# Gate and up blocks of a SwiGLU layer by seven products that add up inside PSUM, the third product of each made during the next block

## The chip, the cores and the metric

The kernel runs on one core of one Trainium2 chip. The metric is device microseconds per execution, the median of three runs; lower is better. Matrix products run on TensorE (PE), elementwise work on VectorE (DVE) and ScalarE (ACT), a few small steps on GpSimd (POOL), and SyncE (SP) issues the loads. PE writes into PSUM, eight banks of 128 x 512 float32; DVE and ACT read them from there.

## The reference

One transformer layer on 512 rows of width 1024 in float32: a token mixer of two kinds of attention, a cross attention into 256 memory rows, and a SwiGLU feed-forward layer (FFN), each between two RMS norms and added to the residual. The change is in the FFN:

```python
D_FF = -(-8 * D_MODEL // 768) * 256          # 2816

def swiglu(h, w_gate_up, w_down):
    g, u = jnp.split(h @ w_gate_up, 2, axis=-1)
    return (jax.nn.silu(g) * u) @ w_down

        h = rms_norm(x, g_ffn_pre[l])
        x = x + rms_norm(swiglu(h, w_gate_up[l], w_down[l]), g_ffn_post[l])
```

## The kernel before

**Precision.** PE multiplies a rounded float32 format. Each operand is therefore split into a high part (a copy that rounds, on ACT) and a low part (the rest, a subtraction on DVE), and each product is three matmuls: high by high, high by low, low by high.

**Stages.** The FFN comes last, from about 425 us on. The normalised input stands transposed in `bt`, as blocks b11, b21, b12, b22 (two halves of the 1024 inner rows by two halves of the 512 rows of x), high and low. The 5632 columns of `w_gate_up` are done in 22 times two pieces of 128 columns each: block n is a gate block if n is even and an up block if odd, of 256 columns (two pieces m), and u = n // 2 counts pairs. Pair 0 comes from weights loaded earlier (`first_ffn`). Blocks 2 to 21 take their weights from a ring in SBUF. Then the down projection runs, first for the left 512 output columns, then for the right; five of its eleven items per half (`SEVEN`, items 4 to 8) are done by seven products too.

**One block.** A block is a 2 x 2 product: weights a11, a21, a12, a22 (two inner halves by two pieces of 128 columns) with b11 to b22. Directly that is eight products of 12 matmuls of 128 x 256 (`eight`). Strassen's scheme in Winograd's form does it with seven (`seven`), with sums of weights s1 to s4 (made on DVE for each block, L951 to L954) and sums of inputs t1 to t4 (made once, L1137 to L1144). Blocks 2, 3 and 11 are done by eight products, the other 17 by seven. In `seven` each of the seven products ends in PSUM by itself, in four banks, two halves each; ACT copies one of them to SBUF (`v`, L1155), and five additions on DVE (L1161, L1162, L1167, L1169, L1171) make the four outputs. Silu runs on ACT piece by piece for a gate block (L1176), and for an up block DVE multiplies with the gate (L1181, L1183). For u of 1, 2, 3 and 10 `keep` then splits the result (ACT L1062, DVE L1063); for the others the split is put off to the down projection (`late_seven`, L1217 to L1225).

**The ring.** `load_raw` brings a raw piece (512 KB, tile `fraw`, three buffers) by a DMA that SP issues when a buffer is free. `fill_from` writes the high part into `ring_hi` (ACT, L924) and the low part into `ring_lo` (DVE, L925). `take` fills ahead as far as the ring's slots allow, and so casts and splits of the next block stand between the sums of this one. Each engine runs its instructions in order.

**Order.** A scheduler gives each engine's instructions their order when the program is built. A split of the first product's matmuls into two halves of 128 columns (`IN_STEP`) is made at u of 1, 2, 4, 6, 8 and 10.

## Time and profile before

| | |
|---|---|
| median of 3 runs | 774.65 us (774.26 to 774.91) |
| profiled execution, first to last instruction | 771.6 us, granted TensorE clock 0.998 |
| PE, DVE, ACT busy | 755.6, 600.3, 429.4 us |
| gate/up blocks from the ring | 455.18 to 648.94 us |
| down projection and the end | 648.94 to 771.60 us |

The profile is of one execution; its span is 3.05 us under the median of the runs, which also count what lies before its first and behind its last instruction. A row of a timeline gives start, duration, engine, line, operation, output and inputs with their shapes; in brackets stands the idle time of the engine just before and what ended it. A matmul's duration includes its way through the array, so the distance of starts, not the duration, says how fast matmuls follow each other. Durations on DVE and ACT overlap a little in the same way.

### The profile page before, as it was taken

To read this page: it belongs to the slowest core of one execution; us is meant where nothing else is said; L and a number is where in the kernel's file an instruction comes from. 1 tells how busy PE (TensorE), PEld (TensorE's weight loads), DVE (VectorE), ACT (ScalarE), POOL (GpSimd) and SP (SyncE) were. 2 spreads that over 40 slices of the span, in tenths; PEclk is the share of its full clock that TensorE was granted. 3 is DMA by queue.
4 is the path that set the end of the run, shared out by engine and by line. 5 is a ranking of instruction groups with operands and counts; after the bars stand their busy time and mean duration, and the time that the engine had idled before them with its cause. 6 is when DMAs were issued, how large, how long until landed. Compare 5 with 4: busy or idle time off the path is not lost.

```text
span 771.6 us, 12900 instructions
## 1 busy us (share of the span) xinstructions
PE 755.6 (98%) x5012; PEld 677.0 (88%) x5012; DVE 600.3 (78%) x1098; ACT 429.4 (56%) x784; POOL 62.5 (8%) x105
## 2 busy tenths in 40 slices
PE   9999999999999999999999999999999999999996
PEld 9977888887778988877778999999999999898985
DVE  8668889789886688545653779999899998987746
ACT  7558889567874457444553625554444446553421
POOL 1001132100321210000002100000000000000001
PEclk9999999999999999999999999999999999999999
DMA  7522023422313725311340202332433332233312
GB/s 273 139 70 68 28 56 97 123 82 82 109 56 112 267 98 197 120 54 56 131 143 27 83 28 83 110 110 82 138 110 110 110 110 90 102 112 108 106 59 109
DMA packets 60749, 80.05 MB, mean 104 GB/s; under 512 B 2705, under 2 KB 43665, under 8 KB 60689
## 3 DMA queue, kind: packets, MB, share of 16 engines
q1 hardware_dynamic: 59264, 74.49, 29.9%
q0 software_dynamic: 1280, 4.72, 1.7%
q8 instruction: 39, 0.64, 0.3%
q14 instruction: 22, 0.17, 0.1%
q10 hardware_dynamic: 144, 0.02, 0.0%
HBM read 77.13 MB, written 2.10 MB: 103 GB/s over the span
## 4 chain that ended last, share of the span: by engine, by line
PE 79%; DVE 9%; ACT 6%; issue 3%; DMA 2%; POOL 1%; DVEq 0%; POOLq 0%; ACTq 0%
PE ps_a L144 12%; PE ps_a L146 12%; PE ps_a L143 12%; PE ps_a L1094 3%; PE ps_a L1097 3%; PE ps_a L1095 3%; PE ps_s L1097 3%; PE ps_s L1094 3%; PE ps_s L1095 3%; PE ps_s L143 2%; PE ps_s L144 2%; PE ps_s L146 2%; PE ps_t L552 2%; PE ps_o L561 2%; PE ps_s L533 1%
## 5 line engine op out<-in xcount | busy, mean ns | idle before, releaser
L924 ACT CAST ring_hi<-fraw 128x1024 fp32r<-128x1024 f32 (+1 forms) x62 | 57.2, 932 | 61.0 <-DVE fraw L1003 17.0
L126 DVE TENSOR_TENSOR lo<-raw,hi 128x1024 fp32r<-128x1024 f32 x56 | 68.2, 1224 | 20.5 <-ACT hi L125 20.3
L925 DVE TENSOR_TENSOR ring_lo<-fraw,ring_hi 128x1024 fp32r<-128x1024 f32 (+1 forms) x62 | 66.5, 1075 | 17.4 <-ACT ring_hi L924 17.1
L146 PE MATMUL ps_a<-hTh,lo 128*128 128x512 f32 x192 | 76.6, 399 | 0.0
L144 PE MATMUL ps_a<-hTl,hi 128*128 128x512 f32 x192 | 75.9, 395 | 0.0
L143 PE MATMUL ps_a<-hTh,hi 128*128 128x512 f32 x192 | 75.8, 395 | 0.0
L125 ACT CAST hi<-raw 128x1024 fp32r<-128x1024 f32 x56 | 57.8, 1048 | 25.3 <-PE ps_a L144 21.2
L924 ACT CAST ring_hi<-sums 128x1024 fp32r<-128x1024 f32 x34 | 35.7, 1049 | 35.5 <-PE ps_t L1095 10.2
L925 DVE TENSOR_TENSOR ring_lo<-sums,ring_hi 128x1024 fp32r<-128x1024 f32 x34 | 41.4, 1219 | 2.1 <-ACT ring_hi L924 2.1
L144 PEld LDWEIGHTS ps_a<-hTl,hi 128*128 128x128 f32 x192 | 36.1, 188 | 6.4
L146 PEld LDWEIGHTS ps_a<-hTh,lo 128*128 128x128 f32 x192 | 36.1, 188 | 6.3
L143 PEld LDWEIGHTS ps_a<-hTh,hi 128*128 128x128 f32 x192 | 36.2, 188 | 5.7
L547 ACT ACTIVATE p<-p,nm 128x128 f32<-128x128 f32 (+1 forms) x64 | 36.1, 565 | 8.1 <-DVE nm L537 7.2
L1094 PE MATMUL ps_a<-b,ring_hi 128*128 128x256 f32 x140 | 39.1, 279 | 0.0
L1097 PE MATMUL ps_a<-b,ring_lo 128*128 128x256 f32 (+1 forms) x146 | 39.0, 274 | 0.0
L1095 PE MATMUL ps_a<-b,ring_hi 128*128 128x256 f32 x140 | 38.7, 276 | 0.0
L1097 PE MATMUL ps_s<-b,ring_lo 128*128 128x256 f32 x128 | 35.3, 276 | 0.0
L1095 PE MATMUL ps_s<-b,ring_hi 128*128 128x256 f32 x128 | 35.3, 276 | 0.0
L1094 PE MATMUL ps_s<-b,ring_hi 128*128 128x256 f32 x128 | 35.3, 276 | 0.0
L554 ACT CAST pth<-ps_t 128x128 fp32r<-128x128 f32 (+1 forms) x64 | 27.0, 424 | 14.5 <-PE ps_t L552 13.7
L555 DVE TENSOR_TENSOR ptl<-ps_t,pth 128x128 fp32r<-128x128 f32 (+1 forms) x64 | 30.7, 487 | 5.0 <-ACT pth L554 3.8
L552 PE MATMUL ps_t<-ident,p 128*128 128x128 f32 x160 | 28.1, 275 | 1.1 <-DVE p L549 0.8
(552 smaller groups left out, 2630.5 us busy)
## 6 DMA issues: line engine op xcount, KB each, us to landing
raw<-in_dram SPq DMA_DIRECT2D x64, 512.0 KB, 3.7
fraw<-in_dram SPq DMA_DIRECT2D x62, 512.0 KB, 3.5
cb<-in_dram SPq DMA_DIRECT2D x8, 256.0 KB, 2.5
xo<-in_dram POOLq DMA_DIRECT2D x4, 512.0 KB, 7.5
out_dram<-yd SPq DMA_DIRECT2D x8, 256.0 KB, 2.0
rawv<-in_dram SPq DMA_DIRECT2D x3, 520.0 KB, 6.5
xt<-in_dram SPq DMA_DIRECT2D x3, 512.0 KB, 6.6
gb<-in_dram POOLq DMA_DIRECT2D x3, 512.0 KB, 4.4
```

What stands on the lines that cost most here:

```text
L125: act.copy(hi[:, j : j + n, :], raw)
L126: dve.tensor_tensor(out=lo[:, j : j + n, :], in0=raw, in1=f32(hi[:, j : j + n, :]), op=ALU.subtract)
L143: pe.matmul(dst, sh, mh, start=first, stop=False)
L144: pe.matmul(dst, sh, ml, start=False, stop=False)
L146: pe.matmul(dst[:, to], sl, mh[:, to], start=False, stop=last)
L547: act.activation(p[:, :n], p[:, :n], AF.Exp, bias=nm, scale=-1.0, accum_out=sm)
L552: pe.transpose(tp[:, k * P : (k + 1) * P], p[:, k * P : (k + 1) * P], ident)
L924: act.copy(h2, v)
L925: dve.tensor_tensor(out=l2, in0=v, in1=f32(h2), op=ALU.subtract)
L1094: pe.matmul(dst, w[0][:, k, :], b[:, 0, k, :], start=first and k == 0, stop=False)
L1095: pe.matmul(dst, w[0][:, k, :], b[:, 1, k, :], start=False, stop=False)
L1097: pe.matmul(dst[:, to], w[1][:, k, :], b[:, 0, k, to], start=False, stop=last and k == 3)
```

## The change

Two more blocks (3 and 11) are done by seven products; only block 2 is still done by eight. That makes 19 of the blocks from the ring where there were 17.

In a block by seven products three of them are now added to each other inside PSUM. The bank x takes a11 b11; ACT copies it out (`early`, L1178); then s2 t2 is added in place; ACT copies the new value (L1184); then s3 t3 is added, and ACT copies that too (u3, L1191). Two products, with t4 and t1, share a bank p45 and b21's product has a bank p2. One addition on DVE (L1192) gives the two outputs of the right half. The seventh product (s4 by b22) is added to p45 one block later, in `finish_seven`, ahead of that block's last product; two additions on DVE (L1168, L1169) then give the two outputs of the left half. `done(0)` and `keep` of a block therefore also come during the next one. For the last block the finishing product stands in the down projection's first item, behind t = 1. The sums t1 to t4 are written in the program ahead of the first pair, no longer behind it. The early copies of a gate block go to a spare row tile (`rrow`), those of an up block to `U[:, :, 0]`, which the up block before it fills its results into for u of 1, 2, 3.

The order of the weights in the ring changes with it: a11, the raw upper half, s2 with s1, then s4 of the block before with s3.

```diff
         def seven_weights(n, c0):
             raw, total = {}, sums[:, n % 2]
-            s2, s4, s3, s1 = (total[:, i] for i in range(4))
+            s2, s1, _, s3 = (total[:, i] for i in range(4))
+            s4 = sums[:, (n + 1) % 2, 2]
+            first, last = n == SEVENS[0], n == SEVENS[-1]
 
             def a11():
                 raw["lower"] = load_raw(w_gate_up, 0, 4, c0, 256)
                 raw["upper"] = load_raw(w_gate_up, 4, 4, c0, 256)
                 return raw["lower"][:, :, :P]
 
-            def s2_s4():
+            def upper_halves():
+                return raw["upper"]
+
+            def s2_s1():
                 lower, upper = raw["lower"], raw["upper"]
                 dve.tensor_tensor(out=s1, in0=lower[:, :, P:], in1=upper[:, :, P:], op=ALU.add)
                 dve.tensor_tensor(out=s2, in0=s1, in1=lower[:, :, :P], op=ALU.add)
+                dve.tensor_tensor(out=s3, in0=lower[:, :, :P], in1=lower[:, :, P:], op=ALU.add)
                 dve.tensor_tensor(out=s4, in0=s2, in1=upper[:, :, :P], op=ALU.add)
-                dve.tensor_tensor(out=s3, in0=lower[:, :, :P], in1=lower[:, :, P:], op=ALU.add)
                 return total[:, 0:2]
 
-            two = dict(c=2, k=4, n=P)
-            item(at := single(), 512, fill_from(at, dict(k=4, n=P), a11))
-            item(at := double(), 1024, fill_from(at, two, s2_s4))
-            item(at := double(), 1024, fill_from(at, two, lambda: raw["upper"], "p c k n -> p k c n"))
-            item(at := double(), 1024, fill_from(at, two, lambda: total[:, 2:4]))
+            def s4_s3():
+                return s3 if first else total[:, 2:4]
+
+            def s4_own():
+                return s4
+
+            one, two = dict(k=4, n=P), dict(c=2, k=4, n=P)
+            item(at := single(), 512, fill_from(at, one, a11))
+            item(at := double(), 1024, fill_from(at, two, upper_halves, "p c k n -> p k c n"))
+            item(at := double(), 1024, fill_from(at, two, s2_s1))
+            if first:
+                item(at := single(), 512, fill_from(at, one, s4_s3))
+            else:
+                item(at := double(), 1024, fill_from(at, two, s4_s3))
+            if last:
+                item(at := double(), 512, fill_from(at, one, s4_own))
...
-        EIGHT = (2, 3, 11)
+        EIGHT = (2,)
+        SEVENS = [n for n in range(2, FB) if n not in EIGHT]
...
+        for f, b in ((f11, b11), (f21, b21)):
+            dve.tensor_tensor(out=f, in0=f32(b[:, 0]), in1=f32(b[:, 1]), op=ALU.add)
+        dve.tensor_tensor(out=f22, in0=f22, in1=f12, op=ALU.subtract)
+        dve.tensor_tensor(out=f12, in0=f11, in1=f12, op=ALU.subtract)
+        dve.scalar_tensor_tensor(out=f11, in0=f22, scalar=-1.0, in1=f11, op0=ALU.mult, op1=ALU.subtract)
+        dve.scalar_tensor_tensor(out=f21, in0=f11, scalar=-1.0, in1=f21, op0=ALU.mult, op1=ALU.subtract)
+        for t, f in ((t4, f21), (t2, f11), (t1, f12), (t3, f22)):
+            put(t, f)
...
-        for t, f in ((t2, f11), (t4, f21), (t3, f22), (t1, f12)):
-            put(t, f)
-
         def twice(a):
             return bass.AP(a.tensor, a.offset, [list(a.ap[0]), [0, 2], list(a.ap[-1])])
 
-        def seven(O, tags, done, parts):
-
-            p17, p26, p35, p4 = (bank(tag) for tag in tags)
-            v = cp.tile([P, 256], F32, tag="v", name="v", bufs=2)
+        unfinished = []
+
+        def finish_seven(w):
+            O, early, x, p45, p2, done, keep_it = unfinished.pop()
+            product(p45[:, right], w, b22, first=False, more=True)
+            dve.tensor_tensor(out=O[:, 0, 0], in0=p2[:, left], in1=early[:, 0], op=ALU.add)
+            dve.tensor_tensor(out=O[:, 1, 0], in0=p45[:, right], in1=early[:, 1], op=ALU.add)
+            done(0)
+            keep_it()
+
+        def seven(O, early, done, keep_it, parts):
+            x, p45, p2 = (bank(tag) for tag in ("t", "s", "a"))
+            u3 = cp.tile([P, 256], F32, tag="v", name="v", bufs=2)
             (a11,) = take()
-            product(p17[:, left], a11, b11, parts=parts)
-            act.copy(v, p17[:, left])
+            product(x[:, left], a11, b11, parts=parts, more=True)
+            act.copy(early[:, 0], x[:, left])
             ((h, l),) = take()
-            product(p26[:, right], (h[:, 0], l[:, 0]), t2)
-            product(p35[:, left], (h[:, 1], l[:, 1]), b22)
+            product(p2[:, left], (h[:, 0], l[:, 0]), b21)
+            product(p45[:, left], (h[:, 1], l[:, 1]), t4, more=True)
             ((h, l),) = take()
-            product(p26[:, left], (h[:, 0], l[:, 0]), b21)
-            dve.tensor_tensor(out=O[:, 0], in0=halves(p26), in1=twice(v), op=ALU.add)
-            dve.tensor_tensor(out=O[:, 1, 0], in0=p35[:, left], in1=O[:, 0, 1], op=ALU.add)
-            done(0, 0)
-            product(p4[:, left], (h[:, 1], l[:, 1]), t4)
+            product(x[:, left], (h[:, 0], l[:, 0]), t2, first=False, more=True)
+            act.copy(early[:, 1], x[:, left])
+            product(p45[:, right], (h[:, 1], l[:, 1]), t1, first=False, more=True)
             ((h, l),) = take()
-            product(p17[:, right], (h[:, 0], l[:, 0]), t3)
-            dve.tensor_tensor(out=O[:, 1, 1], in0=p17[:, right], in1=O[:, 0, 1], op=ALU.add)
-            product(p4[:, right], (h[:, 1], l[:, 1]), t1)
-            dve.tensor_tensor(out=O[:, 0, 1], in0=p4[:, left], in1=O[:, 1, 1], op=ALU.add)
-            done(0, 1)
-            dve.tensor_tensor(out=O[:, 1], in0=twice(p4[:, right]), in1=O[:, 1], op=ALU.add)
-            done(1, 0)
-            done(1, 1)
-
-        def gate_seven(n, m):
-            act.activation(G[:, n, m], G[:, n, m], AF.Silu, scale=(1.0, -1.0)[m])
+            if unfinished:
+                finish_seven((h[:, 0], l[:, 0]))
+                h, l = h[:, 1], l[:, 1]
+            product(x[:, left], (h, l), t3, first=False, more=True)
+            act.copy(u3, x[:, left])
+            dve.tensor_tensor(out=O[:, :, 1], in0=halves(p45), in1=twice(u3), op=ALU.add)
+            done(1)
+            unfinished.append((O, early, x, p45, p2, done, keep_it))
+
+        def gate_seven(m):
+            act.activation(G[:, :, m], G[:, :, m], AF.Silu, scale=(1.0, -1.0)[m])
 
         def up_seven(dst):
-            def done(n, m):
-                if n == 1 and m == 0:
+            def done(m):
+                if m == 0:
                     dve.tensor_tensor(out=dst[:, 0], in0=G[:, :, 0], in1=U[:, :, 0], op=ALU.mult)
-                if n == 1 and m == 1:
+                else:
                     dve.scalar_tensor_tensor(
                         out=dst[:, 1], in0=G[:, :, 1], scalar=-1.0, in1=U[:, :, 1], op0=ALU.mult, op1=ALU.mult
                     )
 
             return done
 
+        def nothing():
+            return None
+
+        gate_early = rrow.rearrange("p (c n) -> p c n", c=2)
+        up_early = U[:, :, 0]
         for u in range(1, FB // 2):
             parts = IN_STEP if u in (1, 2, 4, 6, 8, 10) else WHOLE
             if 2 * u in EIGHT:
-                eight(("a", "a"), gate_eight, parts)
+                eight(("a", "o"), gate_eight, parts)
             else:
-                seven(G, ("a", "a", "a", "o"), gate_seven, parts)
+                seven(G, gate_early, gate_seven, nothing, parts)
             dst = hidden(u)
-            if 2 * u + 1 in EIGHT:
-                eight(("s", "s"), up_eight(dst), WHOLE)
-            else:
-                seven(U, ("s", "s", "t", "t"), up_seven(dst), WHOLE)
-            keep(u, dst)
+            seven(U, up_early, up_seven(dst), lambda u=u, dst=dst: keep(u, dst), WHOLE)
...
-                (w,) = take()
+                last_gate_up = unfinished and half == 0
+                if last_gate_up:
+                    w4, w = take(2)
+                else:
+                    (w,) = take()
                 if half == 0 and i < 4:
                     late_seven(SEVEN[i])
                 for t in range(NT):
                     if half and t == NT - 1 and DOWN[1].index(i) + 1 == DOWN[1].index(SEVEN[0]):
                         cuts.append(384)
                     down(t, i, w, half == 1 and t == NT - 1 and i == body[-1])
+                    if last_gate_up and t == 1:
+                        finish_seven(w4)
```

The diff leaves out the definitions that only move, a `skip_group_check` argument on the matmuls, and `gh`, `gl` as dictionaries.

Three places show how the instructions stand. The first is ACT in a pair of blocks in the middle of the stage. Before, a block's rows hold the ring's casts, one copy of `v`, and Silu in four pieces (of the previous gate block):

```order
L924 CAST ring_hi<-fraw_5440 128x4x2x128
L924 CAST ring_hi<-sums 128x1024
L1155 COPY v<-ps_a_5548 128x256
L924 CAST ring_hi<-fraw_5672 128x512
L924 CAST ring_hi<-sums 128x1024
L1062 CAST g_5544<-U 128x1024
L924 CAST ring_hi<-fraw_5557 128x4x2x128
L1176 ACTIVATE G<-G 128x256
L924 CAST ring_hi<-sums 128x1024
```

Now there are three copies per block out of the one bank (L1178, L1184, L1191), with the casts of the ring between them, and Silu in two pieces:

```order
L924 CAST ring_hi<-sums 128x1024
L924 CAST ring_hi<-fraw_6098 128x512
L1178 COPY rrow<-ps_t_5979 128x256
L924 CAST ring_hi<-fraw_5987 128x4x2x128
L1184 COPY rrow<-ps_t_5979 128x256
L924 CAST ring_hi<-sums 128x1024 x2
L1191 COPY v<-ps_t_5979 128x256
L924 CAST ring_hi<-fraw_6210 128x512
L1178 COPY U<-ps_t_6092 128x256
L1197 ACTIVATE G<-G 128x2x256
```

Bank x is `ps_t` here, and `v` holds u3. Before, the copy of `v` had one place per block; now a cast of the ring stands between any two copies out of x, and the first copy of the next block (into `U`) follows the copy of u3 and the cast of a raw tile.

The second place is DVE around the first `keep` of an up block that is made by seven products before and after: up block 5's result before (`g_5313`), up block 3's now (`g_5167`). Before, `keep` follows the block's own multiplications at once, and the rows behind it belong to the next gate block:

```order
L1171 TENSOR_TENSOR U<-ps_t_5202,U 128x512
L925 TENSOR_TENSOR ring_lo<-sums,ring_hi 128x1024
L1181 TENSOR_TENSOR U<-G,U 128x2x256
L1183 SCALAR_TENSOR_TENSOR U<-G,U 128x2x256
L925 TENSOR_TENSOR ring_lo<-fraw_5438,ring_hi 128x512
L951 TENSOR_TENSOR sums<-fraw_5438,fraw_5440 128x512
L1063 TENSOR_TENSOR g_5313<-U,g_5312 128x1024
L925 TENSOR_TENSOR ring_lo<-sums,ring_hi 128x1024
L1161 TENSOR_TENSOR G<-ps_a_5317,v 128x512
```

Now it stands in the next but one block's time: the finish of block 3 (L1169, L1202), an output sum of block 4 (L1168), the first sum of the weights of block 6 out of two raw tiles (L956), a split, and then `keep`:

```order
L925 TENSOR_TENSOR ring_lo<-fraw_5076,ring_hi 128x4x2x128
L925 TENSOR_TENSOR ring_lo<-sums,ring_hi 128x1024
L1169 TENSOR_TENSOR U<-ps_s_4974,U 128x256
L1202 TENSOR_TENSOR U<-G,U 128x2x256
L1168 TENSOR_TENSOR G<-ps_a_5072,rrow 128x256
L956 TENSOR_TENSOR sums<-fraw_5303,fraw_5305 128x512
L925 TENSOR_TENSOR ring_lo<-sums,ring_hi 128x1024
L1080 TENSOR_TENSOR g_5167<-U,g_5166 128x1024
L1192 TENSOR_TENSOR G<-ps_s_5071,v 128x2x256
```

The sum of two raw tiles (L956, `fraw_5303` and `fraw_5305`) and a split have come to stand ahead of `keep`, and the next up block's early copy into `U` has to wait for `keep`.

The third place is DVE just before the first pair of blocks, around L161, which scales the last row tile for PE's transposes. Before:

```order
L925 TENSOR_TENSOR ring_lo<-fraw_4630,ring_hi 128x1024
L150 TENSOR_SCALAR rs_4573<-ms_4571 128x1
L161 TENSOR_SCALAR y<-mix,rs_4573 128x1024
L181 TENSOR_SCALAR f_4577<-ps_t_4581,gn 128x256
L925 TENSOR_TENSOR ring_lo<-fraw_4914,ring_hi 128x512
L181 TENSOR_SCALAR f_4577<-ps_t_4581,gn 128x256
L181 TENSOR_SCALAR f_4577<-ps_t_4590,gn 128x256 x2
L181 TENSOR_SCALAR f_4578<-ps_t_4599,gn 128x256
L887 TENSOR_TENSOR b_4280<-f_4577,b_4280 128x1024
```

Now:

```order
L925 TENSOR_TENSOR ring_lo<-fraw_4630,ring_hi 128x512
L150 TENSOR_SCALAR rs_4573<-ms_4571 128x1
L925 TENSOR_TENSOR ring_lo<-fraw_4632,ring_hi 128x4x2x128
L161 TENSOR_SCALAR y<-mix,rs_4573 128x1024
L181 TENSOR_SCALAR f_4577<-ps_t_4581,gn 128x256
L181 TENSOR_SCALAR f_4577<-ps_t_4590,gn 128x256
L181 TENSOR_SCALAR f_4577<-ps_t_4581,gn 128x256
L181 TENSOR_SCALAR f_4577<-ps_t_4590,gn 128x256
L887 TENSOR_TENSOR b_4280<-f_4577,b_4280 128x1024
L181 TENSOR_SCALAR f_4578<-ps_t_4599,gn 128x256
L1104 TENSOR_TENSOR f_4579<-b_4279 128x1024
L1104 TENSOR_TENSOR f_4580<-b_4279 128x1024
```

A split of the raw tile `fraw_4632` now stands ahead of L161, and the first two sums of the inputs (L1104) stand between L887, which makes the low part of the first half of `bt[1]`, and the last pieces (L181) of its second half.

More of the change, by code (lines that the diff above doesn't have):

```diff
@@ L1038, in hybrid_block_kernel @@
         U = cp.tile([P, 2, 2, 256], F32, tag="xp", name="U", bufs=2)
-        gh, gl, gf = [], [], []
+        gh, gl, gf = {}, {}, []
         def hidden(u):
@@ L1067, in keep @@
             for b in range(2):
-                gh.append(h[:, b])
-                gl.append(l[:, b])
+                gh[2 * u + b] = h[:, b]
+                gl[2 * u + b] = l[:, b]
         gf_views = {}
@@ L1074, in halves, with put @@
             return a.rearrange("p (t n) -> p t n", t=2)
+        b11, b21, b12, b22 = bt[0][:, 0], bt[0][:, 1], bt[1][:, 0], bt[1][:, 1]
+        t1, t2, t3, t4 = (
+            wp.tile([P, 2, 4, 256], F32R, tag=tag, name=f"t{tag}", bufs=2) for tag in ("hi", "hi", "lo", "lo")
+        )
+        def put(t, f):
+            act.copy(t[:, 0], f)
+            dve.tensor_tensor(out=t[:, 1], in0=f, in1=f32(t[:, 0]), op=ALU.subtract)
+        for f, b in ((f11, b11), (f21, b21)):
[6 more added lines that the diff above has]
+            put(t, f)
         accs = [(bank("a"), bank("s")) for _ in range(2)]
@@ L1088, in hybrid_block_kernel, with product @@
                         )
-        def product(dst, w, b, first=True, last=True, parts=WHOLE):
+        def product(dst, w, b, first=True, last=True, parts=WHOLE, more=False):
             for k in range(4):
@@ L1126, in hybrid_block_kernel @@
         keep(0, hidden(0))
-        t1, t2, t3, t4 = (
-            wp.tile([P, 2, 4, 256], F32R, tag=tag, name=f"t{tag}", bufs=2) for tag in ("hi", "hi", "lo", "lo")
-        )
-        def put(t, f):
-            act.copy(t[:, 0], f)
-            dve.tensor_tensor(out=t[:, 1], in0=f, in1=f32(t[:, 0]), op=ALU.subtract)
-        for f, b in ((f11, b11), (f21, b21)):
-            dve.tensor_tensor(out=f, in0=f32(b[:, 0]), in1=f32(b[:, 1]), op=ALU.add)
-        dve.tensor_tensor(out=f22, in0=f22, in1=f12, op=ALU.subtract)
@@ L1226, in late_seven @@
             put(slice(3, 7), slice(0, 4))
-        gh, gl = ({(k if k < 8 else k + 12): a for k, a in enumerate(g)} for g in (gh, gl))
         def late(u, flat):
```

17 lines of the change are left out of this document (6 added, 11 removed).

## The prediction

> **What bounds the kernel now.** First the page's totals, then a table by stage, then what PE waited for, then the rows around its stops.
>
> ```profile
> span 771.6 us, 12900 instructions
> PE 755.6 (98%) x5012; PEld 677.0 (88%) x5012; DVE 600.3 (78%) x1098; ACT 429.4 (56%) x784; POOL 62.5 (8%) x105
> 455.18:648.94 193.76, 193.76 (x1711) 193.76 (x1710) 181.04 (x255) 95.94 (x141) 0.00 (x0) 1.00 0.32 102
> 670.73:697.00 26.27, 25.22 (x214) 24.76 (x213) 22.27 (x36) 14.00 (x19) 0.00 (x0) 1.00 0.33 110
> PE ps_s L144 <- DVE ring_lo L925: 1.1, 2, 0.6
> ```
>
> The second line names TensorE (PE) as the bound: 98% of the span. The third is the gate/up stage which the change rewrites (columns: length, then busy time of PE, weight load, DVE, ACT, POOL, the clock, DMA share and GB/s). PE is busy for all of its 193.76 us at full granted clock. So there is no stall to win there: time falls only with matmuls, and any new wait of PE is paid in full. DVE is busy 181.04 of it (93%), so it is the engine that could become the next bound; ACT is at 50%. The fourth line, the seven-product part of the down projection, is the only later FFN stage with idle PE (26.27 less 25.22), and the last line says on what: twice on DVE's `ring_lo`.
>
> ```profile
> 464.71:475.59 10.88, 10.88 (x98) 10.88 (x97) 10.03 (x11) 5.79 (x7) 0.00 (x0) 1.00 0.28 90
> 485.24:494.76 9.52, 9.52 (x87) 9.52 (x85) 9.24 (x15) 4.98 (x8) 0.00 (x0) 1.00 0.36 112
> 475.36 0.28 PE L1095 MATMUL ps_s<-b,ring_hi 128*128 128x256 f32 x1
> 475.48 0.28 PE L1097 MATMUL ps_s<-b,ring_lo 128*128 128x256 f32 x1
> 689.72 0.28 PE L146 MATMUL ps_t<-ring_hi,latelo 128*128 128x256 f32 x1
> 689.84 0.28 PE L143 MATMUL ps_t<-ring_hi,latelo 128*128 128x256 f32 x1
> ```
>
> The windows are one eight-product block (96 matmuls) and one seven-product block (84; neighbours at the edges are counted in). 10.88/96 and 9.52/84 give 0.1133 us per matmul of 256 columns, which I call a step; twelve, one product, are a slot of 1.36 us. The matmul pair at 475 has that spacing, rounded; after a stall the same shape runs at 0.1175 or so (689.72 to 689.84), until a product split in two halves puts it back (the kernel splits at u = 1, 2, 4, 6, 8, 10). I call that out of step and price it at 0.0045 us per matmul.
>
> **The change part by part.** *Fewer products.* Blocks 3 and 11 go from eight products to seven: 2 x 12 matmuls x 0.1133 = **-2.72 us**, all on the path. The late finishing product is moved, not added, and the last one lands in the down projection.
>
> *The sums on DVE and ACT.*
>
> ```profile
> 486.28 0.69 DVE L1171 TENSOR_TENSOR G<-ps_o,G 128x512 f32<-128x512 f32 x1
> 486.89 1.22 DVE L925 TENSOR_TENSOR ring_lo<-sums,ring_hi 128x1024 fp32r<-128x1024 f32 x1
> 493.26 0.42 DVE L1162 TENSOR_TENSOR U<-ps_t,U 128x256 f32<-128x256 f32 x1
> 493.60 1.22 DVE L925 TENSOR_TENSOR ring_lo<-fraw,ring_hi 128x1024 fp32r<-128x1024 f32 x1
> 494.73 0.42 DVE L1167 TENSOR_TENSOR U<-ps_s,U 128x256 f32<-128x256 f32 x1
> 487.64 0.36 ACT L1155 COPY v<-ps_s 128x256 f32<-128x256 f32 x1
> L924 ACT CAST ring_hi<-sums 128x1024 fp32r<-128x1024 f32 x34 | 35.7, 1049 | 35.5 <-PE ps_t L1095 10.2 <-PE ps_a L1095 9.2 <-PE ps_s L1095 8.4
> ```
>
> Start to start, back to back, DVE takes 0.61 us for 512 elements, 0.34 for 256, 1.13 for 1024. A seven block's five adds (512, three 256, 512) are 2.24 us; the new three (256, 256, 512) 1.29. The weight sums and splits stay. A pair of blocks took about 18.5 of 19.04 us on DVE (the 93% above, and 9.24 of 9.52 in the block shown) and should take about 16.6, 87%. ACT gains two copies of 0.36 us per block and loses launches of Silu: still under 65%. Neither shows in the time by itself.
>
> *New waits of PE.* The second product into bank x waits for the first early copy on ACT, the third for the second. In each case two other slots lie between: 2.72 us, against a copy of 0.36 and hand-offs. In the block above, ACT had copied `v` long before PE returned to that bank, and the stage shows no PE idle. What can use up the 2.72 us is what stands ahead of the copy in ACT's queue: casts (1.05) that wait for a DMA or for DVE. One such cast and the copy leave 1.3 us of the 2.72, two leave 0.3; from block 6 on the order shows at most one cast between the product and its copy, hence 0 there (0 to 0.1 a block).
>
> The Trainium skill, page "PSUM — Partial Sum Buffer", section "PSUM bank collisions raise a hardware error", speaks against the design: two engines must not be in one bank at once, the hardware does not arbitrate, so software must serialise them by bank. Three products through one bank then cost a turn PE to ACT to PE each; were all 38 turns exposed at 0.36 us, the sum would be 13.7 us worse. The trace sides with the cover: with such a copy in all 17 blocks PE's idle there is 0.
>
> *Block 5* is where I expect the first wait to show. Its early copy goes into `U`, which the previous up block still holds until `keep` (L1080) has run.
>
> ```profile
> fraw<-in_dram SPq DMA_DIRECT2D x37, 512.0 KB, 3.5
> 644.74 4.57 DMA fraw<-in_dram
> L1063 DVE TENSOR_TENSOR g<-U,g 128x1024 fp32r<-128x1024 f32 x3 | 3.7, 1221 | 0.0
> ```
>
> From block 4's start, DVE frees the raw buffer of block 3's split at 1.45 us; DMA 3.5 (the group's median); two sums and a 1024 split to 7.35; that frees the next buffer, DMA 3.5 to 10.85; a sum (0.61), a split (1.13), `keep` (1.13), copy (0.36) to 14.1; PE wants it at 9.52 + 3 x 1.36 = 13.6. With DMAs of 3.5 that is 0.5 us late; with both at 4.57, the slowest shown, 2.6 late. I add four hand-offs of 0.15, an estimate between these ends: **+1.1 us** (0.5 to 2.6). Queued behind the waiting sum on DVE are that split, `keep` and the adds, which PE wants only through this copy. If it leaves PE out of step until block 8 that costs 216 x 0.0045 = 0.97; I cannot tell and take half, **+0.5** (0 to 1.0). Blocks 7 and 9 have the same chain without the DMA: 1.05 + 1.13 + 1.13 + 0.36 = 3.7 of 4.08. I take 0 (0 to 0.5 each).
>
> *Before the first blocks.* The tile preparation (L1104 to L1108) is moved ahead of the first block's sums, and a split of a further raw buffer ahead of L161.
>
> ```profile
> 437.54 0.28 PE L143 MATMUL ps_s<-b,up_hi 128*128 128x256 f32 x1
> 437.66 0.28 PE L144 MATMUL ps_s<-b,up_hi 128*128 128x256 f32 x1
> 451.18 0.34 PE L146 MATMUL ps_a<-b,gate_w 128*128 128x128 f32 x2
> 436.31 0.15 DVE L150 TENSOR_SCALAR rs<-ms 128x1 f32<-128x1 f32 x1
> 437.12 0.75 DVE L161 TENSOR_SCALAR y<-mix,rs 128x1024 f32<-128x1024 f32 x1 [0.66 <-POOL rs L151]
> 442.86 1.22 DVE L887 TENSOR_TENSOR b<-f,b 128x1024 fp32r<-128x1024 f32 x1
> 446.40 1.22 DVE L887 TENSOR_TENSOR b<-f,b 128x1024 fp32r<-128x1024 f32 x1
> ```
>
> L161 had 0.66 us of idle ahead of it; a 1.13 us split there makes it about 0.5 to 0.9 late, and PE's transposes behind it with it. Two adds of 1.13 also come before the second L887. Against that, PE runs out of step here (437.54 to 437.66) up to the split at 451.18; a wait might shift it back (some 115 matmuls, 0.5). **+0.6** (-0.2 to +1.4).
>
> *Into the down projection.* The raw buffers are freed two slots earlier (the upper half is cast first), and DVE is less loaded.
>
> ```profile
> 648.62 0.42 DVE L1167 TENSOR_TENSOR U<-ps_s,U 128x256 f32<-128x256 f32 x1
> 650.47 1.23 DVE L925 TENSOR_TENSOR ring_lo<-fraw,ring_hi 128x1024 fp32r<-128x1024 f32 x1 [1.43 <-ACT ring_hi L924]
> 681.82 1.22 DVE L925 TENSOR_TENSOR ring_lo<-fraw,ring_hi 128x1024 fp32r<-128x1024 f32 x1
> 682.42 0.28 PE L143 MATMUL ps_s<-ring_hi,latehi 128*128 128x256 f32 x1
> 683.10 0.38 PE L144 MATMUL ps_s<-ring_lo,latehi 128*128 128x256 f32 x1 [0.41 <-DVE ring_lo L925]
> 687.87 0.28 PE L143 MATMUL ps_s<-ring_hi,latelo 128*128 128x256 f32 x1
> 688.79 0.39 PE L144 MATMUL ps_s<-ring_lo,latelo 128*128 128x256 f32 x1 [0.65 <-DVE ring_lo L925]
> 696.43 0.28 PE L146 MATMUL ps_o<-ring_hi,latep 128*128 128x256 f32 x1
> ```
>
> DVE lost 1.43 us to a late DMA at the border and reached the split PE needed at 683.04, 34.1 us after the border at 648.94. In the new order I add up what stands between the border and that split: 12 x 1.13 + 12 x 0.61 + 29 x 0.34 = 30.7 us. PE, with the finishing product (1.36) moved in, arrives 35 us after. So three microseconds spare: both stops (the spacings 0.68 and 0.92 less a step of 0.11: 0.57 and 0.81) go, **-1.4**, and the out-of-step run to 696.43, 65 matmuls, **-0.3**. At worst they stay: 0. Next late there is the finishing product's own wait (DVE L1192 of block 21, about 0.3 us to spare): 0 (0 to 0.5).
>
> Sum: -2.72 + 1.1 + 0.5 + 0.6 - 1.4 - 0.3 = **-2.2 us**. The profiled span of 771.6 becomes 769.4; the median of the runs, 774.65, is 3.05 above that span, and I keep the distance: **772.4 us**.
>
> **The rivals.**
> *A, clean:* the waits of block 5 and of the prelude are hidden. For it: chains estimated within 0.5 us of the deadline. -2.72 - 1.7 = -4.4: 770.2.
> *B, eaten:* the new waits appear and the down stops only move, since PE also arrives earlier by the saved time. For it: DVE is saturated there in the trace (22.27 of 26.27). Against: the 3 us counted. -2.72 + 2.2 = -0.5: 774.1.
> *C, slower:* the copies get stuck behind casts that wait for a DMA.
>
> ```profile
> ACT ring_hi L924 <- DMA fraw<-in_dram: 6.0, 5, 2.7
> ```
>
> That happened five times in the old stage, longest 2.7 us. Behind such a cast (0.62) the copy (0.36) comes 3.7 us after its product, 1.0 over the cover; it decides once a cast waits over 1.8 us. Five times 1.0, each with 170 matmuls out of step (0.77), is 8.9; with -2.72, +0.6 and the down gain of -1.7, it ends at +5: 779.7. Against: buffers are freed earlier now, and early copies stand mostly ahead of the cast on a raw tile.
> *D:* the change does not do what it says, no product saved: 774.7. The instruction order has 24 matmuls fewer, so only a small chance.
>
> **How the numbers follow.** Forecast (771.4 to 773.4) 0.42, A 0.20, B 0.24, C 0.12, D 0.02. What a measurement here can tell from no change is 0.2%, 1.55 us: faster means under 773.1. That takes three quarters of the forecast (0.32), all of A and a quarter of B: 0.58; slower is C and a little of B: 0.13; the rest 0.29. The range goes from just under A to past B with block 5 at its upper end (774.1 + 1.5): 770.0 to 776.0, leaving out C and the tails.
>
> **What would show it.** Right: 24 fewer matmuls; in the gate/up stage PE idle of about 1 us at one place, block 5, behind ACT's copy L1178; DVE near 87%; no stop at the down sevens. Wrong: stops at copies in many blocks (C), stops on `ring_lo` in the down part (B), long runs at 0.1175 spacing where none was.

## The result and the profile after

The changed kernel is **slower: 783.71 us** (median of 4 runs, 782.73 to 784.48) against 774.78 (774.26 to 775.11, 4 runs). The ratio is 1.0117, with a 95% interval of 1.0102 to 1.0131. The prediction said 772.4 and faster.

The page of the profiled execution (782.73 us by itself) begins so, with the totals and the engines' busy time:

```profile
span 781.0 us, 12875 instructions
PE 758.2 (97%) x4988; PEld 677.2 (87%) x4988; DVE 594.1 (76%) x1083; ACT 441.7 (57%) x811; POOL 63.7 (8%) x105
```

PE has the 24 matmuls less (4988 for 5012). Its idle time is now 22.8 us of the span, where it was 16.0. The table by stage (columns as in the prediction) says where: first the gate/up stage, then the sevens of the down projection.

```profile
455.19:658.25 203.06, 195.85 (x1685) 193.69 (x1684) 172.00 (x239) 108.18 (x166) 0.00 (x0) 1.00 0.31 98
681.99:706.40 24.41, 24.41 (x215) 24.32 (x214) 19.76 (x31) 11.71 (x17) 0.00 (x0) 1.00 0.38 121
```

The gate/up stage took 193.88 us before, from the last matmul of the first pair to the first of the down projection, and takes 203.06 now; 7.2 of that PE is idle. The sevens of the down projection have lost their idle time.

I split the 9.4 us between the spans at five points, by PE's starts. Where the distance of two starts is over 0.2 us longer than the 0.1133 us of a matmul, the surplus counts as a stop; any smaller surplus counts as out of step, also the 0.11 us that follows each stop.

| stretch | before | after | change |
|---|---|---|---|
| up to the first matmul of the FFN | 427.68 | 428.60 | +0.92 |
| first pair and blocks from the ring | 221.26 | 229.65 | +8.39 |
| first part of the down projection | 21.79 | 23.74 | +1.95 |
| its sevens, left half | 25.82 | 23.92 | -1.90 |
| the rest, to PE's last matmul | 67.57 | 67.57 | 0 |

In the second row, 36 matmuls fewer are -4.08 (two products, and the finishing product that moves into the next row); stops in the blocks are +8.67 (none before), and out of step is +3.57 (4.39 against 0.82). The first pair took 27.38 us and takes 26.59, but nine of the ring's matmuls (1.02 us) no longer fall into its time, so it is 0.23 worse. The first row lies ahead of the FFN and varies between 427.9 and 428.9 in the kernels below, so part of it is not the change's.

What PE waited for, and a row of the same view for DVE (engine, output, line, what it waited for: us in total, times, longest):

```profile
PE ps_t L1129 <- ACT U L1178: 3.7, 3, 2.1
PE ps_t L1129 <- ACT rrow L1178: 1.8, 2, 0.9
PE ps_s L1132 <- DVE ring_lo L925: 1.6, 3, 0.6
DVE sums L956 <- DMA fraw<-in_dram: 17.9, 8, 3.1
```

PE waits for the early copies on ACT and for DVE's splits. The last row is the one that matters: DVE stood for 17.9 us in front of the sum s1 (L956), which needs a raw piece that has not landed. In the kernel before, the same sum waited little:

```profile
DVE sums L951 <- DMA fraw<-in_dram: 3.2, 4, 1.8
```

What queues behind that sum is seen in DVE's timeline (start, duration, line, operation, output and inputs; in brackets the idle time just before and its end):

```profile
565.34 0.42 DVE L1168 TENSOR_TENSOR G<-ps_a,rrow 128x256 f32<-128x256 f32 x1
568.83 0.69 DVE L956 TENSOR_TENSOR sums<-fraw,fraw 128x512 f32<-128x512 f32 x1 [3.07 <-DMA fraw<-in_dram]
569.44 0.69 DVE L1192 TENSOR_TENSOR G<-ps_s,v 128x512 f32<-128x512 f32 x1
570.04 1.22 DVE L925 TENSOR_TENSOR ring_lo<-sums,ring_hi 128x1024 fp32r<-128x1024 f32 x1
...
576.19 0.42 DVE L1169 TENSOR_TENSOR G<-ps_s,rrow 128x256 f32<-128x256 f32 x1
579.63 0.69 DVE L956 TENSOR_TENSOR sums<-fraw,fraw 128x512 f32<-128x512 f32 x1 [3.03 <-DMA fraw<-in_dram]
580.24 0.68 DVE L1192 TENSOR_TENSOR U<-ps_s,v 128x512 f32<-128x512 f32 x1
```

L956 is the sum of block n + 3, which PE needs more than a block later; L1192 makes the outputs of block n, and ring splits follow it. The scheduler set L956 ahead of L1192 for five n (4, 12, 13, 16 and 17), and five of the eight waits, 13.0 of the 17.9 us, are at these sums. In the rows above DVE does nothing for 3 us each time, although L1192's inputs are there (the second time for the last 2 us). ACT then waits for L1192 with a Silu, and the rest of its queue waits with it:

```profile
570.16 0.64 ACT L1197 ACTIVATE G<-G 128x512 f32<-128x512 f32 x1 [3.24 <-DVE G L1192]
570.70 1.03 ACT L924 CAST ring_hi<-fraw 128x1024 fp32r<-128x1024 f32 x1
...
573.58 1.22 DVE L925 TENSOR_TENSOR ring_lo<-fraw,ring_hi 128x1024 fp32r<-128x1024 f32 x1
```

The second row is the high part of a raw piece, and the third is DVE's split of it. Only when the split is done is that raw buffer free, and only then can the DMA start for which the next L956 waits. The high part was ready 1.85 us before the split began, so it is DVE's own queue, late by its wait, that frees the buffer late. So the wait feeds itself. The chain of work that ended last (start, us, what) shows a split, the DMA behind it, the sum, and what stood behind the sum:

```profile
601.83 0.68 DVE gf L1204
602.52 1.21 DVE ring_lo L925 x2
...
606.06 1.15 DVE ring_lo L925
607.22 4.80 DMA fraw<-in_dram
612.12 0.13 DVE sums L956
...
612.73 0.68 DVE G L1192
613.41 1.14 DVE ring_lo L925
614.60 0.39 PE ps_s L1132
```

From one such L956 to the next pass 10.80 us (568.83 to 579.63; likewise 612.12 to 622.97, 10.85), and PE at full pace needs 9.52 for a block. So PE stops about once a block there. By its brackets it stops seven times after block 5: three times at a split of DVE (571, 604 and 615 us) and four times at an early copy. These rows show the two kinds of late copy:

```profile
576.64 0.63 ACT L1197 ACTIVATE G<-G 128x512 f32<-128x512 f32 x1 [3.69 <-DVE G L1169]
579.32 0.39 PE L1129 MATMUL ps_t<-thi,ring_hi 128*128 128x256 f32 x1 [0.91 <-ACT rrow L1178]
...
632.58 0.62 ACT L924 CAST ring_hi<-fraw 128x512 fp32r<-128x512 f32 x1 [3.01 <-DMA fraw<-in_dram]
633.52 0.38 PE L1129 MATMUL ps_t<-thi,ring_hi 128*128 128x256 f32 x1 [0.82 <-ACT U L1178]
```

At 579 and 623 the copy stands behind a Silu that waited for DVE's L1169, the second addition of the left half. At 590 and 633 it stands behind one cast of a raw piece that had waited 3.01 us. The profile puts the wait at 590 down to PE, but there too the piece had landed only 0.07 us before the cast.

### The profile page after: what moved, and what is told of

Its sections match the earlier page's. It is cut to its first block, busy times and chain, and to the rows that moved or that the text cites. A ratio compares the mean times of both kernels' runs of the same rounds, so it can differ in the third digit from the quotient of the medians.

```text
span 781.0 us, 12875 instructions
## 1 busy us (share of the span) xinstructions
PE 758.2 (97%) x4988; PEld 677.2 (87%) x4988; DVE 594.1 (76%) x1083; ACT 441.7 (57%) x811; POOL 63.7 (8%) x105
## 4 chain that ended last, share of the span: by engine, by line
PE 76%; DVE 9%; ACT 6%; DMA 4%; issue 3%; POOL 1%; DVEq 0%; POOLq 0%; ACTq 0%
PE ps_a L144 13%; PE ps_a L146 13%; PE ps_a L143 13%; DMA fraw<-in_dram 3%; DVE ring_lo L925 3%; PE ps_t L1129 2%; PE ps_s L143 2%; PE ps_s L144 2%; PE ps_s L146 2%; PE ps_t L1132 2%; PE ps_t L1130 2%; PE ps_s L1129 2%; PE ps_s L1132 2%; PE ps_s L1130 2%; PE ps_t L552 2%
## 5 line engine op out<-in xcount | busy, mean ns | idle before, releaser
L924 ACT CAST ring_hi<-sums 128x1024 fp32r<-128x1024 f32 (+1 forms) x39 | 40.1, 1029 | 39.6 <-PE ps_s L1130 16.2
L925 DVE TENSOR_TENSOR ring_lo<-sums,ring_hi 128x1024 fp32r<-128x1024 f32 (+1 forms) x39 | 46.6, 1194 | 8.1 <-ACT ring_hi L924 8.0
L1129 PE MATMUL ps_t<-thi,ring_hi 128*128 128x256 f32 x76 | 21.9, 288 | 5.6 <-ACT U L1178 3.7
L549 DVE TENSOR_SCALAR p<-p,rc 128x128 f32<-128x128 f32 (+1 forms) x64 | 26.8, 419 | 0.1
L956 DVE TENSOR_TENSOR sums<-fraw,fraw 128x512 f32<-128x512 f32 x19 | 13.1, 690 | 17.9 <-DMA fraw<-in_dram 17.9
L552 PEld LDWEIGHTS ps_t<-ident,p 128*128 128x128 f32 x160 | 19.3, 140 | 7.3 <-issue 2.4
L1132 PE MATMUL ps_a<-b,ring_lo 128*128 128x256 f32 (+1 forms) x93 | 25.5, 276 | 0.0
L1129 PE MATMUL ps_a<-b,ring_hi 128*128 128x256 f32 x92 | 25.5, 278 | 0.0
```

The source lines that it names most:

```text
L552: pe.transpose(tp[:, k * P : (k + 1) * P], p[:, k * P : (k + 1) * P], ident)
L924: act.copy(h2, v)
L925: dve.tensor_tensor(out=l2, in0=v, in1=f32(h2), op=ALU.subtract)
L1129: pe.matmul(dst, w[0][:, k, :], b[:, 0, k, :], start=first and k == 0, stop=False, skip_group_check=more)
L1132: pe.matmul(dst[:, to], w[1][:, k, :], b[:, 0, k, to], start=False, stop=last and k == 3, skip_group_check=more,)
```

## The experiments

The theory at this point: the time is lost because L956 stands ahead of L1192 in DVE's queue. The rivals: too few raw buffers; the early copy of an up block, which must wait for `keep`; the turn from PE to ACT and back in one bank, which the design adds; and too many blocks by seven products, whichever scheme they use. Medians are given with their range and number of runs. All runs of the kernel before in the same jobs had medians between 774.3 and 775.1.

### Undo the order alone: e1_behind

A copy of one column makes s1 of block n + 3 come behind L1192 of block n. It reads that output and writes into the place that s1 then overwrites.

```diff
             dve.tensor_tensor(out=O[:, :, 1], in0=halves(p45), in1=twice(u3), op=ALU.add)
+            if n + 3 < FB:
+                dve.tensor_copy(out=sums[:, (n + 1) % 2, 1, 0, :1], in_=O[:, 0, 1, :1])
             done(1)
```

> The changed kernel, but the first sum of the raw tiles for block n + 3 (L956) is made to stand behind block n's output sum L1192 on DVE (a 128x1 copy ties the two; nothing else moves by hand). Theory A (DVE stands in order at L956 for a transfer whose data PE needs only one and a half blocks later, with L1192 and a split behind it): the stops of PE between 570 and 640 us, 6.7 us together, go, and DVE's wait for the DMA at L956 falls from 17.9 to under 6 us: 777 us (775.5 to 779). Theory B (three raw buffers are the bound, 10.8 us a block in whatever order): DVE waits for the same transfers one instruction later, 783 to 784.5. Theory C (the turn from PE to ACT's copy and back is itself too slow): no change, 783 to 784.5.

Measured: **772.0 us** (771.76 to 772.79, 6), ratio 0.9965 [0.9952, 0.9977]. Nothing is taken away, one small instruction per block is added, and 11.7 us go. The gate/up stage in the table by stage, DVE's wait and a part of its timeline:

```profile
455.21:647.26 192.05, 192.05 (x1685) 192.05 (x1684) 173.49 (x255) 108.93 (x166) 0.00 (x0) 1.00 0.33 103
```

```profile
DVE sums L956 <- DMA fraw<-in_dram: 0.3, 1, 0.3
```

```profile
571.87 0.69 DVE L1192 TENSOR_TENSOR U<-ps_s,v 128x512 f32<-128x512 f32 x1 [0.96 <-ACT v L1191]
572.60 0.15 DVE L1194 COPY sums<-U 128x1 f32<-128x1 f32 x1
...
575.61 0.68 DVE L956 TENSOR_TENSOR sums<-fraw,fraw 128x512 f32<-128x512 f32 x1
```

PE has no idle time in the stage, and DVE waits for a DMA once, 0.3 us, with the same three raw buffers. L956 comes 3.7 us behind L1192 and finds its data there. So the order is shown to be the cause of most of the loss; the DMA was late because the order made it late. The scheduler was free to place other instructions anew as well, so what is shown is the new order as a whole, with this one dependency as all that was put in.

### More raw buffers: e2_buf4 and e5_behind_buf4

Every fourth raw tile of the gate and up weights goes to a spare tile, so that four can be under way. First in the changed kernel, then together with e1's copy.

```diff
-            raw = wp.tile([P, nkb, ncol], F32, tag="raw", name=f"fraw{raws[0]}", bufs=3)
+            if w is w_gate_up and raws[0] > 6 and raws[0] % 4 == 0:
+                raw = cp.tile([P, nkb, ncol], F32, tag="up", name=f"fraw{raws[0]}")
+            else:
+                raw = wp.tile([P, nkb, ncol], F32, tag="raw", name=f"fraw{raws[0]}", bufs=3)
```

> The changed kernel with a fourth raw buffer for every fourth raw tile of the gate and up weights; the scheduler may reorder. Theory A: transfers land before DVE stands at L956, most of its 17.9 us of waiting goes: 776 to 779. Theory B: the loop through the buffers gets a third longer lead, all stops between 570 and 640 go: 776 to 778. Theory C: no change, 783 to 784.5.

> e1 (L956 of block n + 3 tied behind L1192 of block n) together with e2's fourth raw buffer. Theory A (order alone): with the order right there is no wait for the buffer to shorten, 771.5 to 772.5, like e1; e2's 786 then came from the scheduler's putting that sum ahead of L1192 (L1195 there) in every block. Theory B (buffers count too): below 771, or, if the tile in the other pool does harm by itself, 780 and more.

Measured: alone **786.0** (784.9 to 787.93, 4), ratio 1.0147 [1.013, 1.0165]; with the order mended **771.27** (770.99 to 771.83, 4), ratio 0.9956 [0.9942, 0.9971]. The first result was not what I expected, and does not answer its question, since the scheduler moved with it. The waits of DVE in e2_buf4 (the sum is L959 there):

```profile
DVE sums L959 <- DMA fraw<-in_dram: 23.3, 12, 3.1
```

With a fourth buffer the sum of every block from block 6 on (block n + 3) was placed ahead of L1195, the addition that makes block n's outputs there, and DVE waited 12 times, not 8. With the order held fixed, the buffer was worth 0.7 us between medians, with overlapping intervals. Buffers were not the bound.

### The early copy in a tile of its own: e3_early

```diff
-        up_early = U[:, :, 0]
+        up_early = cp.tile([P, 2176], F32, tag="up", name="up_early")[:, 1024:1536].rearrange("p (c n) -> p c n", c=2)
```

> The changed kernel, the up blocks' early copies in a tile of their own and no longer in U, so that they do not wait for keep (L1080). If block 5's stop (2.2 us by spacing, at 489.96) comes from that wait, it goes, and the time is 781.5 (781 to 782.2), the stops after 570 as before. If the copy was late through ACT's queue or the transfer, the stop stays: 783 to 784.5.

Measured: **778.32** (777.77 to 779.86, 4), ratio 1.0049 [1.0034, 1.0064], 5.4 us under the changed kernel, which is more than I expected. PE's waits and DVE's:

```profile
PE ps_t L1129 <- ACT rrow L1178: 2.4, 3, 1.0
PE ps_t L1129 <- ACT up_early L1178: 1.8, 2, 0.9
PE ps_s L1132 <- DVE ring_lo L925: 1.5, 2, 0.9
```

```profile
DVE sums L956 <- DMA fraw<-in_dram: 17.8, 8, 3.3
```

The stop of 2.05 us in block 5 is gone, but DVE's wait is as long as it was, and the later stops stay. The profiled execution was the slowest of the four; in it the blocks took 3.2 us less than in the changed kernel. Of these 3.2 us, 1.7 are stops and 1.5 is time out of step. So the copy's tile is a part of the loss (2.9 us between the spans, 5.4 between the medians), and not its main cause.

### The number of blocks by seven products alone: e4_before19

The kernel before, with only the list of blocks changed. The scheme is the old one.

```diff
-        EIGHT = (2, 3, 11)
+        EIGHT = (2,)
```

> The kernel before with blocks 3 and 11 by seven products too, in its old scheme: the number of blocks alone. If 24 matmuls fewer are worth their slots and nothing else moves: 772 (771.7 to 772.5). If two more sevens make DVE the bound there (it was at 93%): 774.5 to 777.

Measured: **779.92** (777.3 to 781.16, 4), ratio 1.0062 [1.004, 1.0083]. That is above what either expectation gave. The old scheme loses with 19 such blocks too. What PE waited for:

```profile
PE ps_s L1097 <- DVE ring_lo L925: 2.2, 4, 1.2
PE ps_a L1097 <- DVE ring_lo L925: 2.0, 2, 1.5
```

PE waits for DVE's splits, and DVE is busy for 609.7 us in all, 15.6 more than in the changed kernel. But ACT's casts also waited 36.5 us for a DMA in this kernel (10.7 in the kernel before), so a late DMA has a part in it, and this run doesn't separate DVE's load from the order. That the larger number pays only with fewer additions on DVE is likely, and not shown.

### The order mended only from block 12 on: e6_from12

```diff
-            if n + 3 < FB:
+            if 12 <= n + 3 < FB:
```

> e1 with the tie only for the sums of blocks 12 and later; up to block 11 the order is the changed kernel's. If each stop comes from its own block's order, block 5's stop (2.2 us, near 490) stays with its out-of-step stretch (0.4 to 1.0) and all stops after 560 are gone: 774.2 to 775.4. If the tie acts in another way (DVE's load, a shift that runs through), the stop at 490 goes too or the later ones come back: 772, or 779 and more.

Measured: **775.45** (773.55 to 776.01, 10), ratio 1.0006 [0.9996, 1.0015]. That is 3.45 us above e1 between medians, just over the expected range, and 1.8 between the profiled executions, of which e6's was its fastest. In its profile the one stop left among the blocks is block 5's, and no stop is left after that. The wait, and DVE's rows there:

```profile
PE ps_t L1129 <- ACT U L1178: 2.2, 1, 2.2
```

```profile
486.05 0.69 DVE L956 TENSOR_TENSOR sums<-fraw,fraw 128x512 f32<-128x512 f32 x1 [1.76 <-DMA fraw<-in_dram]
486.66 1.22 DVE L925 TENSOR_TENSOR ring_lo<-sums,ring_hi 128x1024 fp32r<-128x1024 f32 x1
487.79 1.22 DVE L1080 TENSOR_TENSOR g<-U,g 128x1024 fp32r<-128x1024 f32 x1
```

So block 5's stop and the later ones are the same kind of fault in different blocks: a sum that waits for a DMA in front of something due sooner, here in front of `keep` and the copy that needs it.

### The turn between PE and ACT: e7_copies_x3

e1's kernel with each early copy made three times over.

```diff
-            act.copy(early[:, 0], x[:, left])
+            for _ in range(3):
+                act.copy(early[:, 0], x[:, left])
...
-            act.copy(early[:, 1], x[:, left])
+            for _ in range(3):
+                act.copy(early[:, 1], x[:, left])
```

> e1 with each early copy (L1178, L1184) made three times over, 0.5 to 0.7 us more on ACT between two products into bank x, 38 times. If two other products cover the turn with about 1.3 us to spare (the prediction's step): 772 to 773. If the turn is at its edge (theory C): 0.5 us 38 times, up to 790.

Measured: **772.42** (772.18 to 772.87, 7), ratio 0.997 [0.9959, 0.9981]; with 76 more copies the time moves by 0.4 us (1.0 between the profiled spans). The waits of PE on the copies:

```profile
PE ps_t L1129 <- ACT U L1179: 1.6, 3, 0.8
```

Three stops, in blocks 5, 7 and 9, where `keep` stands ahead of the copy. In the other 16 blocks the cover of two slots holds even three copies. That is also what became of the rule of the Trainium skill that the prediction weighed (page "PSUM — Partial Sum Buffer", section "PSUM bank collisions raise a hardware error": two engines must not be in one bank at once). The turns are made, as the rule demands, and with the order mended they cost PE no idle time in these blocks.

### The sums of the inputs behind the first pair again: e8_sums_late

e1's kernel, with the whole piece that makes t1 to t4 moved back to where it stood before the change.

```diff
-        for f, b in ((f11, b11), (f21, b21)):
...
-        for t, f in ((t4, f21), (t2, f11), (t1, f12), (t3, f22)):
-            put(t, f)
...
         keep(0, hidden(0))
 
+        for f, b in ((f11, b11), (f21, b21)):
...
+        for t, f in ((t4, f21), (t2, f11), (t1, f12), (t3, f22)):
+            put(t, f)
```

> e1 with the sums of the inputs (L1104 to L1108 and their splits) written behind the first pair again, as in the kernel before. The prediction priced the move at +0.6: then 771.4. By the stage times the move took 0.8 us off the first pair's stage, and without it block 3 finds its sums late, as in e4 (28.57 against 27.38 us for the first pair's stage): 774 to 775.

Measured: **773.89** (772.73 to 774.73, 10), ratio 0.9987 [0.9978, 0.9996], 1.9 us above e1. The rows of PE's waits that e1 does not have:

```profile
PE ps_t L1117 <- ACT rrow L1179: 1.0, 1, 1.0
PE ps_s L1118 <- DVE tlo L1149: 0.9, 1, 0.9
```

The early place saves these two waits.

### Order and own tile together: e9_behind_early and e10_behind_early_buf4

e1's copy and e3's tile together; then a fourth buffer as well. This one begins with the twelfth raw tile, not with the eighth as in e2 and e5, and lies in the same spare tile as the early copies.

> The changed kernel with the sums tied behind L1192 in every block (as in the run that did that alone, 772.0 us) and with the up blocks' early copies in a tile of their own, so that no early copy waits for keep. The own tile alone, without the tie, was worth 5.4 us (778.3 against 783.7), far more than the block 5 stop of about 2 us. Theory (the own tile's gain came from the order that the scheduler chose with it, and from the stop in block 5, and both are already gone with the tie): 771.5 to 772.3, no stop of PE between 455 and 648. Rival (waiting for keep costs something in each of blocks 5, 7 and 9 for itself, hidden in the tied kernel as PE being out of step, 2.37 us of surplus spacing there): 770 to 771.

> As the run before in this job, with a fourth raw buffer too (every fourth raw tile). It is meant as the best version: theory, as the tied kernel with the fourth buffer, 771.0 to 771.6, since buffers were worth 0.7 us with the order right and the own tile nothing. Rival (both add up to something more): under 770.5.

Measured: **769.77** (769.42 to 770.01, 5), ratio 0.9939 [0.9926, 0.9953], and **770.06** (769.71 to 770.37, 5), ratio 0.9943 [0.9931, 0.9956]. The theory fell, and the rival's mechanism held, at a time a little below its range: the own tile is worth something with the order mended too, 2.2 us between the medians. Of the 2.0 us between the profiled spans, 0.7 lie ahead of the FFN, where nothing was changed. The fourth buffer then adds nothing: the gate/up stage of both profiles takes 190.82 us. That is 1.23 us shorter than e1's, all of it busy:

```profile
454.48:645.30 190.82, 190.82 (x1685) 190.82 (x1684) 173.41 (x255) 108.68 (x166) 0.00 (x0) 1.00 0.33 103
```

Most of it begins with one row of ACT in e1, block 9:

```profile
525.69 0.37 ACT L1178 COPY U<-ps_t 128x256 f32<-128x256 f32 x1 [0.75 <-DVE g L1080]
```

It ends at 526.06. PE's first matmul that needs it starts at 526.15, and the next one at 526.34, 0.19 us later and not 0.11: 0.08 us lost, too short for a row among the waits. The copies of blocks 5 and 7 wait for `keep` in the same way and cost PE 0.07 us each, at 488 and 507; behind these PE is back at 0.1133 us within six matmuls. Behind the one of block 9 e1 is out of step up to a split product at 552; e9, whose copy waits for nothing, is not. One product each, by the first rows of two products that follow each other, in e1 and then in e9:

```profile
527.64 0.28 PE L1129 MATMUL ps_s<-thi,ring_hi 128*128 128x256 f32 x1
...
529.05 0.28 PE L1129 MATMUL ps_s<-b,ring_hi 128*128 128x256 f32 x1
```

```profile
525.24 0.28 PE L1129 MATMUL ps_t<-thi,ring_hi 128*128 128x256 f32 x1
...
526.60 0.28 PE L1129 MATMUL ps_s<-thi,ring_hi 128*128 128x256 f32 x1
```

1.41 us against 1.36. That is 0.05 in 1.41 over 26 us, or 0.9 of the 1.23, behind a delay of 0.08. Why PE fell out of step there and not behind the other two is open.

## Why the prediction was wrong

**The step that failed** is "from block 6 on the order shows at most one cast between the product and its copy, hence 0". I looked in ACT's queue alone, and priced what stands ahead of a copy by its own duration (1.05 us) and not by what it waits for. At two of the four late copies there was just one cast ahead, and it had waited 3.0 us for a raw piece. At the other two there was a Silu, which had waited 3.7 us for DVE's L1169. Both go back to DVE's queue, where sums that waited for a DMA stood ahead of the additions, the splits and the freeing of the buffers; the other three stops are at DVE's splits. The seven stops have 5.1 us of idle time in their brackets (6.45 by spacing, with an eighth), and PE was out of step for 3.6 more than before where I had 0.5. The instruction order that I had shows L956 ahead of L1192 in five blocks; for block 4 it is the second of the three places shown (its L956 is the sum of block 7, not of block 6 as said there). I did not ask, of each DVE instruction ahead of L1192, what it waits for. e1 shows that the order was worth 11.7 us.

**"Neither shows in the time by itself."** DVE's load fell, but by less than worked out: a pair of blocks takes 17.1 to 17.3 us of DVE in e1, where 16.6 was forecast and 18.5 was taken before. In the stage it is 172.00 of 203.06 us, 85%, and 173.49 of 192.05 in e1, 90%, against 93%. (The prediction put 18.5 of 19.04 beside the 93%; it is 97%, and the stage has lighter blocks too.) But free time on an engine that works in order is no cover when an early instruction blocks it; it became 17.9 us of waiting.

**Block 5** stopped where I said and by the chain I laid out (sum, split, `keep`, copy), for 2.05 us (2.22 by spacing) against 1.1 (0.5 to 2.6). Behind it PE was back in step within six matmuls, so the 0.5 for out of step did not come there. I took it for an edge case of the ramp, with the DMA's duration as the unknown. e1 and e6 show that it is the same fault of order.

**Blocks 7 and 9** at 0 held for stops. The delay of 0.08 us in block 9 and the time out of step behind it cost 1.0 us in e1, over the 0.5 that I allowed.

**The first pair** was forecast 0.6 worse (-0.2 to +1.4): it is 0.23 worse. PE did wait for L161, as forecast, but only 0.3 us.

**The down projection** was right: both stops on `ring_lo` are gone, -1.90 against -1.7 forecast. (The terms leave 4 us to spare and not the three that I wrote; nothing hangs on it.) The finishing product brings its own 1.36 and a wait of 0.28, which is 0.55 by spacing and so a little over the 0 to 0.5 forecast. **The products**, 24 matmuls or -2.72, were right too.

**The distance** of a run to its span is 1.77 to 1.80 us in the profiled executions of all the later kernels, not the 3.05 that I kept, which compared one execution's span with the median of others. The forecast doesn't hang on it, as it is the median before less 2.2 either way.

**The rivals.** C, slower at 779.7, had the sign, and at two of the seven stops its mechanism: a copy behind a cast that waited 3.0 us for a raw piece, over the 1.8 that it gave as its limit. It did not have the source. ACT's waits for a DMA at its casts (7.3 us in five, 10.7 in nine before) are no longer in all than they were; DVE's waits at the sum made the pieces late and held the splits and the Silu as well. Both reasons against C failed. Buffers were not free early while the order held, since the wait at the sum grew from 3.2 to 17.9 us. And the early copy L1178 does not stand ahead of the cast on a raw tile: in the order shown ahead of the prediction it stands right behind one, both times. A, clean at 770.2, is about what e9 reaches (769.77) once the two obstacles are taken away.

**What stays open.** Why the scheduler placed the sum ahead in some blocks and not in others was not tried; that the choice shifts with small things is seen in e2. How much of a DMA's landing time (4.80 us in the chain above) is transfer and how much is waiting behind the transfer ahead of it was not measured.

## What to carry to other kernels

Read the new order on every engine for instructions that wait for a DMA, and ask what stands behind each one that is due sooner; an engine with idle time can still be the cause. Where a scheduler sets the order, a change can let it start an operation too early; a cheap false dependency puts it back, and it is worth trying before a good idea is dropped: here 783.7 became 772.0 with it, and 769.8 with a tile of its own for the early copies. More buffers do not mend an order, and may change it for the worse.

## What the runs showed of the hardware

Behind one delay of 0.08 us PE ran at 0.1175 us instead of 0.1133 per matmul for the next 26 us, which cost some ten times the delay (e1 against e9). This is no rule: behind two delays of 0.07 us in the same kernel PE recovered within six matmuls, as it did in the changed kernel behind the stops at 490 and 579, while behind the one at 571 it stayed out of step until the next. A stop need not show among the waits to matter; the spacing has to be read.

The loop did not show at first. From 529 to 554 PE ran out of step in the changed kernel too, at about 9.9 us a block, and DVE's sum waited for nothing; the stops began at 571, after a split product had set PE back to 9.52. That the slower pace had hidden the loop is likely; no run tests it.
